# All gated output rows of the mixers as seven block products, in another order of the seven

## The chip, the cores and the metric

The kernel runs on one core of a Trainium2 chip. The metric is the device time of one execution in microseconds (us). Engines are named as in the profile: PE (matrix multiplies; PEld is its weight load), DVE (vector), ACT (scalar: copies, casts and activations), POOL (here mostly DMA issue) and SP (DMA issue). Each engine works through its own instructions in order and waits at semaphores for the others.

## The reference, cut to what matters

The program is one step of a two-layer encoder on 640 rows (512 prompt frames and 8 x 16 sample frames), in fp32. A layer is a feed-forward half step, a mixer, and a second feed-forward half step. The change lies in the mixer:

```python
z = h @ w_in                      # h: 640 x 1024; columns: conv B, C, V | q, k, v | gates
g = sigmoid(z[gates] + b_gate)    # 2048 gate columns
g_conv, g_attn = split(g, 2)
m = g_conv * (y_conv @ w_conv_out) + g_attn * (y_attn @ w_attn_out)   # y: 640 x 512, w: 512 x 1024
x = x + m @ w_o
```

## The kernel before, in words

Everything is kept transposed: 128 features on the partitions, the 640 rows along the free dimension, in two halves `t1` and `t2` of 320. A fp32 product is made of three fp32r matmuls: weights and operands are each split into `hi` (an ACT cast to fp32r) and `lo` (a DVE subtraction), and `hi*hi`, `hi*lo`, `lo*hi` are summed in PSUM.

**Products by seven.** For the gates, the kernel takes the weights of a pair of output blocks and a pair of input blocks as a 2 x 2 matrix, the activations (two input blocks by two halves) as another, and forms the 2 x 2 product with seven block products instead of eight. The seven are named by their operand: `11`, `21`, `22` are quarters of the activations as they are; `N6`, `T5`, `T7`, `T4` are differences of quarters. A unit of this kind ("mix") reads two weight tiles of 128 x 1024 and turns them into four slabs: slab 0 holds the weights of products 11 and 21, slab 1 those of N6 (first half, from sums `s`) and T5 (second half, from `raw`), slab 2 those of T7 (`one`, which POOL adds up by DMA) and 22, slab 3 those of T4. Per unit PE issues 7 x 12 matmuls of 320 columns, 84 in all.

**Stage.** The function `outputs` is the last part of each mixer, after attention, and is run once for each of the two layers. Its instructions on PE, DVE and ACT stand in the order in which the code is written (`tc.manual_schedule` with all three engines), so that order is what each engine follows. It consists of gate pairs `gate_pair(2)` to `gate_pair(14)` (seven units by seven), and of the gated output rows between them: 8 rows of `co` (conv) and 8 of `ao` (attention). Rows 4 to 7 of each are made by `rows`, one unit by seven for four output rows. Rows 0 to 3 are made singly by `out`: four plain products on the operands `yc` or `ya`, 24 matmuls, into one PSUM tile `py`. After the stage, the `w_o` products `po` read its result `mo`.

**Weights run ahead.** `prep(i)` has ACT cast slab `i` into `whi`; `flush()` has DVE form `wlo`. `slab()` hands out the next slab and prepares the one two further on; `quiet()` hands one out and prepares nothing. `source()` has DVE add up raw tiles (`raw`, `s`) where a slab is a sum. There are three buffers each of `whi` and `wlo`.

**Names in the trace.** `qa`, `qb`, `qc` are the three PSUM banks of a gate pair: bank a takes 11, then N6, T7 and T4; b takes 21; c takes T5, then 22. ACT copies bank a out after 11 (`capsm`, below "copy c1") and after N6 (`capsm` again, "copy u2"), and bank c after T5 (`c`). Only then may N6, T7 and 22 add to those banks. `ra..`, `rb..`, `rc..` are the same for `rows`, with copies into `capsm` or `rs`; the copy of bank a after N6 is `rs<-raco`. `rrm` is the norm's factor, `g` the gates, `mm` the output rows, `sm` the gate bias of the sigmoids (`ACTIVATE g<-g,sm`). Sigmoids are held back in `lates` and issued by `due()` after copy c1 of the next unit.

The two functions that the diff touches, `mixer_order` (the order of the weights in memory) and `outputs`:

Of the kernel before, what the change touches and what calls it, by code (L numbers as in the profile page):

```python
# [16 lines left out]
P = 128  # L17
# [170 lines left out]
def two(ps):  # L188
    return ps[:, :, :HT]
# [7 lines left out]
def trunk(ctx: ExitStack, tc: tile.TileContext, xin, wst, small, pbias, samplebias, kcache, vcache, gfin,  # L197
# [1299 lines left out]
    def outputs(l, gp, X, st, cs, ycp, yas, sigmoid, gates):  # L1497
# [4 lines left out]
        ycs = [z[:, i] for z in ycp for i in range(2)]  # L1502
        mm = [spare[i // 2][:, i % 2] for i in range(CT)] + ycs
# [14 lines left out]
        def gate_pair(m, at):  # L1518
# [6 lines left out]
            u, g = gates[m], gates[m + 1] = tmp(f"g{n}"), tmp(f"g{n}_1")  # L1525
            prep(used[0] + 1)
            flush()
            at[0]()
# [8 lines left out]
            at[1]()  # L1537
# [6 lines left out]
            at[2]()  # L1544
# [8 lines left out]
            block(pa, s3, 0, XT4, every, False, True)  # L1553
            DVE.tensor_tensor(out=g[:, t1], in0=pa, in1=rr[:, t1], op=ALU.mult)
            lates.append(lambda: sigmoid(g, m + 1, -1.0))
            flush()

        def parts(pool, tag, name, src):
            hi, lo = (pool.tile([P, T], F32R, tag=f"{tag}{i}", name=f"{name}{i}") for i in ("hi", "lo"))
            split(hi, lo, src)  # L1560
            return hi, lo

        def out(m, y, then=None, post=None):

            due()
            py = acc(f"py{l}_{m}")
            product(py, y)
            if then:
                then()
            g = gates[m]  # L1570
            if m < KT:
                DVE.tensor_tensor(out=halves(mm[m]), in0=two(py), in1=halves(g), op=ALU.mult)
            else:
                DVE.tensor_tensor(out=halves(g), in0=two(py), in1=halves(g), op=ALU.mult)
                add(mm[m - KT], mm[m - KT], g)
            flush()
            if post:
                post()

        yc, ya = [], []  # L1580
        mo = [None] * KT
        srcs = [yas[:, c, :] for c in range(CT)]
        x, moves = {}, []

        def take(y, name, cs, srcs):
            for c in cs:
                y.append(parts(gp, f"y{c}", f"{name}{l}_{c}", srcs[c]))

        def take_even(c):
            y = tuple(gp.tile([P, T], F32R, tag=f"y{c}{i}", name=f"ya{l}_{c}{i}") for i in ("hi", "lo"))  # L1590
            split(*(z[:, t1] for z in y), srcs[c][:, t1])
            ya.append(y)

        def low(lo, z, hi):
            DVE.tensor_tensor(out=lo, in0=z, in1=hi.bitcast(F32), op=ALU.subtract)

        def room(name):
            for k in EXTRA:
                x[name, k] = tuple(gp.tile([P, 2, HT], F32R, tag=f"x{EXTRA.index(k)}{i}",
                                           name=f"x{i}{name}{l}_{EXTRA.index(k)}") for i in ("hi", "lo"))  # L1600

        def minus(out, a):
            DVE.scalar_tensor_tensor(out=out, in0=a, scalar=-1.0, in1=out, op0=ALU.mult, op1=ALU.subtract)

        def mixed(i):

            z = ycp[i].rearrange("p c (a b) -> p (c a) b", a=2)
            e1, e2, o1, o2 = (z[:, k] for k in range(4))
            add(e1, e1, e2, ALU.subtract)
            add(e2, o2, e2, ALU.subtract)  # L1610
            minus(o2, e1)
            minus(o1, o2)
            yield
            for k in EXTRA:
                ACT.copy(x["co", k][0][:, i], z[:, 1 + EXTRA.index(k)])
            yield
            for k in EXTRA:
                hi, lo = (u[:, i] for u in x["co", k])
                low(lo, z[:, 1 + EXTRA.index(k)], hi)
            yield  # L1620
            hi, lo = (u[:, t2] for u in yc[2 * i])
            ACT.copy(hi, e1)
            yield
            low(lo, e1, hi)
            yield

        za = yas.rearrange("p (i c) (a b) -> p i (c a) b", i=2, a=2)

        def mix(n):

            e1, e2, o1, o2 = (za[:, :, k] for k in range(4))
            if n == 0:
                add(e1, e1, e2, ALU.subtract)
            elif n == 1:
                add(e2, o2, e2, ALU.subtract)
            else:
                minus(*((o2, e1) if n == 2 else (o1, o2)))

        def place(k):
            if k == XT5:  # L1640
                return [(*(u[:, t2] for u in ya[2 * i]), za[:, i, 0]) for i in range(2)]
            return [(*x["ao", k], za[:, :, 1 + EXTRA.index(k)])]

        def high(*ks):
            for k in ks:
                for hi, _, z in place(k):
                    ACT.copy(hi, z)

        def rest(*ks):
            for k in ks:  # L1650
                for hi, lo, z in place(k):
                    low(lo, z, hi)

        EXTRA = XT7, XT4, XN6

        def kind(name, i, k):
            if k in EXTRA:
                return tuple(z[:, i] for z in x[name, k])
            hi, lo = (yc if name == "co" else ya)[2 * i + (k in (X21, X22))]
            return tuple(z[:, t2 if k in (X22, XT5) else t1] for z in (hi, lo))  # L1660

        def rows(name, ms, first, mid=None, late=None, end=False, defer=False):

            n = f"{name}{l}_{ms[0]}"
            gs = [gates[m + (KT if name == "ao" else 0)] for m in ms]
# [3 lines left out]
            s1, s2, s5 = stage  # L1669

            def mul(ps, s, half, k, start):
                for u in range(2):
                    for i in range(2):
                        kp = half * NP + 2 * u + i
                        wh, wl = (z[:, kp * P : (kp + 1) * P] for z in s)
                        xh, xl = kind(name, i, k)
# [13 lines left out]
            def moved(r):  # L1690
                for u in range(2):
                    ACT.copy(mm[ms[2 * r + u]], gs[2 * r + u])

            w = quiet()
            mul(a, w, 0, X11, True)
            ACT.copy(s1, two(A))
# [8 lines left out]
            flush()  # L1705
            mul(a, w, 0, XN6, False)
            ACT.copy(s2, two(A))
            gated(0, [s1[:, u] for u in range(2)], t1)
            if mid:
                mid()  # L1710
            mul(c, w, 1, XT5, True)
            for u in range(2):
                ACT.copy(s5[:, u], c[u])
            w = slab(True)[0]
            mul(a, w, 0, XT7, False)
# [3 lines left out]
            if defer:  # L1719
                moves.append(lambda: gated(1, [s5[:, u] for u in range(2)], t2, -1.0))  # L1720
            else:
                gated(1, [s5[:, u] for u in range(2)], t2, -1.0)
            if late:
                late()
            mul(c, w, 1, X22, False)
# [4 lines left out]
            mul(a, w, 0, XT4, False)  # L1730
# [3 lines left out]
            if name == "co":  # L1734
                lates.append(lambda: moved(0))
                moves.append(lambda: moved(1))
            if end:
                flush()

# [12 lines left out]
        none = lambda: None  # L1752

        def going(*zs):
            return lambda: [next(z) for z in zs]

        gate_pair(2, [none, none, lambda: take(yc, "yc", range(CT), ycs)])
        z = [mixed(i) for i in range(2)]
        room("co")
        out(0, yc, None, going(z[0]))  # L1760
        out(1, yc, None, going(*z))
        out(2, yc, None, going(*z))
        out(3, yc, None, going(z[1]))
        gate_pair(4, [going(*z), going(*z), none])
        gate_pair(6, [none] * 3)
        rows("co", (4, 5, 6, 7), None)
        gate_pair(8, [none, moves[0], lambda: take(ya, "ya", range(CT), srcs)])
        room("ao")
        out(8, ya, None, lambda: mix(0))
        out(9, ya)  # L1770
        gate_pair(10, [lambda: mix(1), lambda: (mix(2), high(XT7)), lambda: (mix(3), rest(XT7))])
        out(10, ya)
        out(11, ya)
        gate_pair(12, [none, lambda: high(XN6, XT4), lambda: (rest(XN6, XT4), high(XT5))])
# [664 lines left out]
```

## Time and profile before

| what | value |
|---|---|
| median of 3 runs (lowest, highest) | 2481.88 us (2481.07 to 2482.76) |
| span of the profiled execution | 2479.9 us |
| busy: PE, DVE, ACT, POOL | 99%, 88%, 56%, 13% of the span |
| HBM read | 239.48 MB |

The profiled execution's own time is its span, from the first instruction to the last; the timed runs lie 2.0 us above it at the median. "Busy" counts a time in which at least one instruction of the engine was under way. Matmuls overlap, so that PE at 99% says that PE hardly ever stood still, and nothing of how full it was.

### The profile page before, as it was taken

The numbers are of one execution on the slowest core, as the hardware profiler recorded it, in microseconds if no ns is written. First come the engines' busy times: TensorE is split into PE (matmuls) and PEld (weight loads), VectorE is DVE, ScalarE is ACT, GpSimd is POOL, SyncE is SP. The second block draws the span as 40 slices with busy tenths as digits, with TensorE's granted clock in tenths as the row PEclk, the third lists the DMA queues.
The fourth block names the chain that finished last, engine by engine and source line by source line (L and its number), as shares of the span: only waits on it lengthen the run. The fifth ranks groups of instructions, "written<-read, shape, count | busy, mean of one in ns | idle before, by whom it ended". The sixth has DMA issues, their size and how long they took to land.

```text
span 2479.9 us, 44056 instructions
## 1 busy us (share of the span) xinstructions
PE 2466.4 (99%) x17264; PEld 2414.6 (97%) x17264; DVE 2182.6 (88%) x3644; ACT 1386.7 (56%) x2231; POOL 320.8 (13%) x483
## 2 busy tenths in 40 slices
PE   9999999999999999999999999999999999999999
PEld 8999999889999999999999999998899999999998
DVE  7999998888888899998799999988888889999997
ACT  6555555665555555555665555566655556555555
POOL 0211112211000001111001010121110000111111
PEclk9999999999999999999999999999999999999999
DMA  4443444335344234444334343452453432444444
GB/s 155 128 120 101 124 117 120 114 110 175 102 118 123 93 102 107 112 118 119 109 94 109 110 117 102 117 128 102 138 167 94 119 119 92 108 113 107 112 117 117
DMA packets 113520, 288.16 MB, mean 116 GB/s; under 512 B 12992, under 2 KB 52544, under 8 KB 113312
## 3 DMA queue, kind: packets, MB, share of 16 engines
q1 hardware_dynamic: 69552, 220.10, 27.0%
q0 software_dynamic: 43328, 64.99, 13.8%
q8 instruction: 135, 2.21, 0.4%
q14 instruction: 73, 0.60, 0.1%
q10 hardware_dynamic: 432, 0.25, 0.0%
HBM read 239.48 MB, written 7.94 MB: 100 GB/s over the span
## 4 chain that ended last, share of the span: by engine, by line
PE 91%; DVE 4%; issue 3%; ACT 1%; DMA 1%; DVEq 0%; SPq 0%; ACTq 0%; POOLq 0%
PE pab L459 12%; PE paa L459 10%; PE pcb L459 6%; PE daa L1147 5%; PE dab L1147 5%; PE pca L459 5%; PE po L435 5%; PE qa L459 4%; PE pbb L459 3%; PE dca L1147 3%; PE dcb L1147 2%; PE pba L459 2%; PE ma_cv L459 2%; PE ma_qk L459 2%; PE py L435 2%
## 5 line engine op out<-in xcount | busy, mean ns | idle before, releaser
L364 ACT CAST whi<-raw 128x1024 fp32r<-128x1024 f32 (+1 forms) x578 | 502.3, 874 | 373.4 <-PE pbb L459 46.3
L369 DVE TENSOR_TENSOR wlo<-raw,whi 128x1024 fp32r<-128x1024 f32 (+1 forms) x578 | 577.0, 1001 | 135.4 <-ACT whi L364 131.2
L364 ACT CAST whi<-s 128x1024 fp32r<-128x1024 f32 (+1 forms) x162 | 152.9, 944 | 319.4 <-DVE s L296 113.5
L459 PE MATMUL pab<-xhib,whi 128*128 128x320 f32 x704 | 217.7, 309 | 0.0
L459 PE MATMUL pab<-xhib,wlo 128*128 128x320 f32 x704 | 217.2, 309 | 0.0
L459 PE MATMUL pab<-xlob,whi 128*128 128x320 f32 x704 | 217.2, 309 | 0.0
L459 PE MATMUL paa<-xhia,whi 128*128 128x320 f32 x640 | 197.8, 309 | 0.2 <-DVE ga L296 0.2
L459 PE MATMUL paa<-xhia,wlo 128*128 128x320 f32 x640 | 197.5, 309 | 0.0
L459 PE MATMUL paa<-xloa,whi 128*128 128x320 f32 x640 | 197.5, 309 | 0.0
L369 DVE TENSOR_TENSOR wlo<-s,whi 128x1024 fp32r<-128x1024 f32 (+1 forms) x162 | 176.3, 1088 | 4.0 <-ACT whi L364 4.0
L1169 POOL DMA_DIRECT2D x<-c_a x80 | 69.9, 1021 | 575.9 <-ACT ahia L1051 205.5
L1169 POOL DMA_DIRECT2D x<-c_b x72 | 63.2, 1014 | 583.1 <-ACT ahib L1051 205.4
L459 PEld LDWEIGHTS pab<-xhib,whi 128*128 128x128 f32 x704 | 132.1, 188 | 0.9 <-issue 0.9
L459 PEld LDWEIGHTS pab<-xhib,wlo 128*128 128x128 f32 x704 | 132.1, 188 | 0.0
L459 PEld LDWEIGHTS pab<-xlob,whi 128*128 128x128 f32 x704 | 132.1, 188 | 0.0
L459 PEld LDWEIGHTS paa<-xhia,whi 128*128 128x128 f32 x640 | 120.1, 188 | 1.1 <-DVE ga L296 0.4
L459 PEld LDWEIGHTS paa<-xloa,whi 128*128 128x128 f32 x640 | 120.1, 188 | 0.3 <-DVE xloa L703 0.3
L459 PEld LDWEIGHTS paa<-xhia,wlo 128*128 128x128 f32 x640 | 120.1, 188 | 0.1
L296 DVE TENSOR_TENSOR raw<-s,raw 128x512 f32<-128x512 f32 x162 | 110.7, 683 | 0.0
L459 PE MATMUL pcb<-xhib,wlo 128*128 128x320 f32 x352 | 108.8, 309 | 0.0
L459 PE MATMUL pcb<-xlob,whi 128*128 128x320 f32 x352 | 108.6, 309 | 0.0
L459 PE MATMUL pcb<-xhib,whi 128*128 128x320 f32 x352 | 108.6, 309 | 0.0
(909 smaller groups left out, 8201.3 us busy)
## 6 DMA issues: line engine op xcount, KB each, us to landing
raw<-in_wst SPq DMA_DIRECT2D x375, 512.0 KB, 3.5
x<-c_a POOLq DMA_DIRECT2D x80, 160.0 KB, 4.8
x<-c_b POOLq DMA_DIRECT2D x72, 160.0 KB, 4.2
lent<-in_wst POOLq DMA_DIRECT2D x36, 256.0 KB, 3.7
kc<-in_kcache SPq DMA_DIRECT2D x32, 256.0 KB, 4.8
vc<-in_vcache SPq DMA_DIRECT2D x16, 512.0 KB, 4.3
one<-in_wst POOLq DMA_DIRECT2D x32, 256.0 KB, 4.0
x<-u_a POOLq DMA_DIRECT2D x40, 160.0 KB, 4.1
```

The source lines that it names most:

```text
L296: DVE.tensor_tensor(out=out, in0=a, in1=b, op=op)
L364: ACT.copy(hi[:, d], src[:, c])
L369: DVE.tensor_tensor(out=lo, in0=src, in1=hi.bitcast(F32), op=ALU.subtract)
L435: PE.matmul(ps[:, a, :HT], w, x[a] if isinstance(x, tuple) else x[:, a * HT : (a + 1) * HT], start=first and j == 0 and not seeded, stop=l ...
L459: PE.matmul(ps, a, b, start=start and kp == 0 and j == 0, stop=stop and kp == NP - 1 and j == 2, skip_group_check=True)
L1147: PE.matmul(ps[u], w, y, start=start and i == 0 and j == 0, stop=i == 1 and j == 2, skip_group_check=True)
L1169: POOL.dma_start(x[ms[2 * u + r]][:, cols], z[:, u], accum_op=ALU.add)
```

## The change

Rows 0 to 3 of `co` and `ao` are made by `rows` too, so that `out`, its plain products and its operands are gone. `rows` takes the seven in the order 11, T5, N6, 21, T7, 22, T4 (before: 11, 21, N6, T5, T7, 22, T4). It takes slab 1 with `quiet()`, and its weights of slab 3 are cast after product 21. In every `rows` but a layer's first, ACT writes product 11 into bank b, and 21 is added to it there ("seeds a bank"), in place of an addition by DVE. The operands of both groups are made by a class `Mixed`, in eight steps, handed to the gate pairs and the first `rows` of the group as hooks `at[0..3]`: after the cast of slab 2, after the copies u2 and c, before product 22, and at the end. In `gate_pair`, `flush()` now stands ahead of the last product with `rrm`. The sums `total(0..3)` of conv and attention rows move into gate pairs 12 and 14. Gates 2, 3, 6 and 7 are written into the tiles of the output rows, so that two of the four rows' copies `moved` fall away.

```diff
@@ mixer_order
-    out += gates[:2] + [("co", m) for m in range(4)] + gates[2:4] + [("rows", ("co", (4, 5, 6, 7)))]
-    for i in range(2):
-        out += [gates[4 + i], ("ao", 2 * i), ("ao", 2 * i + 1)]
-    out += gates[6:] + [("rows", ("ao", (4, 5, 6, 7)))]
+    rows = [("rows", (name, ms)) for name in ("co", "ao") for ms in ((0, 1, 2, 3), (4, 5, 6, 7))]
+    out += gates[:3] + rows[:1] + gates[3:4] + rows[1:2] + gates[4:6] + rows[2:3] + gates[6:] + rows[3:]
@@ outputs, gate_pair
             prep(used[0] + 1)
             flush()
-            at[0]()
+            call(at, 0)
             block(pb, s0, 1, X21, every, True, True)
...
             block(pa, s3, 0, XT4, every, False, True)
+            flush()
             DVE.tensor_tensor(out=g[:, t1], in0=pa, in1=rr[:, t1], op=ALU.mult)
             lates.append(lambda: sigmoid(g, m + 1, -1.0))
-            flush()
+            call(at, 3)
@@ outputs, class Mixed (new)
+            def high(self, i, *whats):
+                for what in whats:
+                    hi, _, z = self.part(i, what)
+                    ACT.copy(hi, z)
+            def low(self, i, *whats):
+                for what in whats:
+                    hi, lo, z = self.part(i, what)
+                    DVE.tensor_tensor(out=lo, in0=z, in1=hi.bitcast(F32), op=ALU.subtract)
+            def mix(self, i, *ks):
...
+            def steps(self):
+                hi, lo, mix = self.high, self.low, self.mix
+                return [[f] for f in (
+                    lambda: (mix(0, "T5"), hi(0, "11", "T5"), lo(0, "11")),
+                    lambda: (mix(1, "T5"), hi(1, "11", "T5"), lo(0, "T5")),
+                    lambda: (lo(1, "11", "T5"), hi(0, "2")),
+                    lambda: (lo(0, "2"), hi(1, "2")),
+                    lambda: (mix(0, "N6"), hi(0, "N6"), lo(1, "2")),
+                    lambda: (mix(1, "N6"), hi(1, "N6"), lo(0, "N6"), mix(0, "T7", "T4")),
+                    lambda: (lo(1, "N6"), hi(0, "T")),
+                    lambda: (mix(1, "T7", "T4"), hi(1, "T"), lo(0, "T"), lo(1, "T")))]
@@ outputs, rows
             w = quiet()
-            mul(a, w, 0, X11, True)
-            ACT.copy(s1, two(A))
+            mul(a, w, 0, "11", True)
+            ACT.copy(two(B) if seed else s1, two(A))
             due()
             prep(used[0] + 1)
             flush()
-            if first:
-                first()
-            mul(b, w, 1, X21, True)
-            add(s1, two(B), s1)
-            w = slab(True)[0]
-            flush()
-            mul(a, w, 0, XN6, False)
-            ACT.copy(s2, two(A))
-            gated(0, [s1[:, u] for u in range(2)], t1)
-            if mid:
-                mid()
-            mul(c, w, 1, XT5, True)
+            call(at, 0)
+            w1 = quiet()
+            mul(c, w1, 1, "T5", True)
             for u in range(2):
                 ACT.copy(s5[:, u], c[u])
+            mul(a, w1, 0, "N6", False)
+            ACT.copy(s2, two(A))
+            mul(b, w, 1, "21", not seed)
+            prep(used[0] + 1)
+            if not seed:
+                add(s1, two(B), s1)
+            gated(0, b if seed else [s1[:, u] for u in range(2)], t1)
+            flush()
+            call(at, 1)
             w = slab(True)[0]
-            mul(a, w, 0, XT7, False)
+            mul(a, w, 0, "T7", False)
...
@@ outputs, the stage's order
+        yc = Mixed("co", [quarters(z) for z in ycp])
+        at = yc.steps()
+        gate_pair(2, at[:4])
+        gate_pair(4, at[4:7])
+        rows(yc, (0, 1, 2, 3), at[7:])
+        gate_pair(6)
+        rows(yc, (4, 5, 6, 7))
+        ya = Mixed("ao", [quarters(yas[:, 2 * i : 2 * i + 2]) for i in range(2)])
+        at = ya.steps()
+        gate_pair(8, at[:4])
+        gate_pair(10, at[4:7])
+        rows(ya, (0, 1, 2, 3), at[7:])
+        gate_pair(12, [[lambda: total(0)], [lambda: total(1)], [lambda: total(2)]])
+        gate_pair(14, [[lambda: total(3)], [lambda: (begun(*range(4)), given(0, 2))]])
+        rows(ya, (4, 5, 6, 7), [[], [lambda: given(1, 3)]], True)
```

How the instructions stand, at three places of the first layer.

PE, where product 11 of `rows` for co rows 4 to 7 ends (weights `whi_7802` and `wlo_7803` are slab 0), before:

```order
L1678 MATMUL raco_4_7862<-yc_2lo,whi_7802 128x320
L1678 MATMUL raco_4_7862<-yc_2hi,wlo_7803 128x320
L1678 MATMUL rbco_4_7861<-yc_1hi,whi_7802 128x320
L1678 MATMUL rbco_4_7861<-yc_1lo,whi_7802 128x320
L1678 MATMUL rbco_4_7861<-yc_1hi,wlo_7803 128x320
```

The same place after (`whi_7813`, `wlo_7814` are slab 0, `whi_7852` and `wlo_7853` slab 1):

```order
L1643 MATMUL raco_4_7873<-y1co_1lo,whi_7813 128x320
L1643 MATMUL raco_4_7873<-y1co_1hi,wlo_7814 128x320
L1643 MATMUL rcco_4_0_7874<-y4co_0hi,whi_7852 128x320
L1643 MATMUL rcco_4_0_7874<-y4co_0lo,whi_7852 128x320
L1643 MATMUL rcco_4_0_7874<-y4co_0hi,wlo_7853 128x320
```

The second of the seven now reads slab 1, 12 matmuls after the unit's start, where before it read slab 0 again.

ACT, in gate pair 8, from copy c1 to the copy of bank c, before (`whi_8019` is slab 2, `whi_8038` slab 3):

```order
L1523 COPY capsm_4819<-qa_8_7998 128x320
L1692 COPY yc_0_4821<-g_4_7613 128x640
L1692 COPY yc_0_4821<-g_4_1_7614 128x640
L364 CAST whi_8019<-one_7822 128x512
L364 CAST whi_8019<-raw_7933 128x512
L364 CAST whi_8038<-raw_7952 128x512
L1534 COPY capsm_4819<-qa_8_7998 128x320
L1536 COPY c_4831<-qc_8_8000 128x320
```

After (`y1ao_0hi`, `y4ao_0hi` are operands of products 11 and T5):

```order
L1525 COPY capsm_4819<-qa_8_8020 128x320
L1657 COPY yc_0_4821<-g_4_0_7478 128x640
L1657 COPY yc_0_4821<-g_4_1_7479 128x640
L362 CAST whi_8041<-one_7833 128x512
L362 CAST whi_8041<-raw_7943 128x512
L1592 CAST y1ao_0hi<-ya_4762 128x320
L1592 CAST y4ao_0hi<-ya_4762 128x320
L362 CAST whi_8064<-raw_7962 128x512
L1536 COPY capsm_4819<-qa_8_8020 128x320
L1538 COPY c_4831<-qc_8_8022 128x320
```

Two operand casts stand between the casts of slabs 2 and 3 and so ahead of copy u2; the second of them reads what DVE mixes in the same step.

ACT, from the end of gate pair 2 into the next unit, before (the next unit is the plain products `out`):

```order
L364 CAST whi_7425<-raw_7394 128x1024
L1354 ACT_TABLE_LOAD
L1354 ACTIVATE g_0_7126<-g_0_7126,sm 128x640
L1354 ACTIVATE g_1_7127<-g_1_7127,sm 128x640
L1354 ACTIVATE g_2_7324<-g_2_7324,sm 128x640
```

After (the next unit is gate pair 4, and `capsm<-qa_4` its copy c1):

```order
L362 CAST whi_7436<-s_94_7417 128x512
L362 CAST whi_7436<-raw_7412 128x512
L1352 ACT_TABLE_LOAD
L1352 ACTIVATE g_0_7126<-g_0_7126,sm 128x640
L1352 ACTIVATE g_1_7127<-g_1_7127,sm 128x640
L1592 CAST y2co_1hi<-yc_1_4822 128x640
L1525 COPY capsm_4819<-qa_4_7460 128x320
```

The load of the sigmoids' table, two sigmoids and an operand cast now stand right ahead of a copy that product N6 waits for.

More of the change, by code (lines that the diff above doesn't have):

```diff
@@ L1580, in outputs @@
[L1580 to L1642, printed above, removed]
@@ L1666, in rows @@
+        seeded = [False]
+        def rows(y, ms, at=(), end=False):
+            n = f"{y.name}{l}_{ms[0]}"
+            co = y.name == "co"
+            gs = [gates[m + (0 if co else KT)] for m in ms]
             B, A = (acc(f"r{i}{n}") for i in "ba")
@@ L1718, in rows @@
             ahead()
[L1719 to L1725, printed above, removed]
+            gated(1, [s5[:, u] for u in range(2)], t2, -1.0)
+            call(at, 2)
+            mul(c, w, 1, "22", False)
             for u in range(2):
@@ L1750, in given, with quarters @@
                 split(*mo[m], mm[m])
[L1752 to L1774, printed above, removed]
-        pre = lambda: rest(XT5)
-        gate_pair(14, [pre, lambda: (begun(*range(4)), given(0, 2)), none])
-        rows("ao", (4, 5, 6, 7), None, lambda: given(1, 3), None, True)
+        def quarters(z):
+            return z.rearrange("p c (a b) -> p (c a) b", a=2)
+        yc = Mixed("co", [quarters(z) for z in ycp])
[13 more added lines that the diff above has]
+        rows(ya, (4, 5, 6, 7), [[], [lambda: given(1, 3)]], True)
         begun(*range(4, KT))
```

97 lines of the change are left out of this document (49 added, 48 removed).

## The prediction

> **What bounds the kernel now.** I read the page first, then the stage `outputs` of each layer (product 11 of gate pair 2 to the first `po`), then groups, then single transitions.
>
> ```profile
> span 2479.9 us, 44056 instructions
> PE 2466.4 (99%) x17264; PEld 2414.6 (97%) x17264; DVE 2182.6 (88%) x3644; ACT 1386.7 (56%) x2231; POOL 320.8 (13%) x483
> PE 91%; DVE 4%; issue 3%; ACT 1%; DMA 1%; DVEq 0%; SPq 0%; ACTq 0%; POOLq 0%
> one<-in_wst POOLq DMA_DIRECT2D x32, 256.0 KB, 4.0
> ```
>
> PE is busy for 99% of the span and is 91% of the chain that ended last. So a matmul less counts in full, and so does any wait of PE that is new. The windows show the stage in both layers:
>
> ```profile
> core 0: us, PE busy (x) PEld busy (x) DVE busy (x) ACT busy (x) POOL busy (x), PEclk, DMA share, GB/s
> 635.00:774.30 139.30, 139.25 (x950) 138.95 (x949) 120.73 (x195) 79.91 (x133) 8.60 (x12) 1.00 0.36 106
> 1863.56:2002.82 139.26, 139.21 (x950) 138.91 (x950) 120.59 (x195) 79.76 (x133) 8.64 (x12) 1.00 0.35 107
> ```
>
> PE never rests, at clock 1.00. The code has 9 units of 84 matmuls and 8 `out` of 24, 948 in all (the windows touch two more): 139.30 / 948 = 0.147 us each, 1.76 for a block of 12, 12.34 for a unit. DVE rests for 18.6 us of the stage, ACT for 59.4. The layers agree within 0.04 us, so I work out the first and double it.
>
> **What falls away.** Per layer 8 x 24 matmuls go and 2 x 84 come: 24 fewer, 24 x 0.147 = 3.53 us. One wait that PE has now goes with the old order; it also shows what a late `wlo` costs (gate pair 14, product N6):
>
> ```profile
> 752.60 0.68 DVE L369 TENSOR_TENSOR wlo<-s,whi 128x512 fp32r<-128x512 f32 x1
> 752.97 0.31 PE L459 MATMUL qa<-tlo,whi 128*128 128x320 f32 x1
> 753.33 0.41 PE L459 MATMUL qa<-thi,wlo 128*128 128x320 f32 x1
> ```
>
> `wlo` ends at 753.28, the matmul that reads it starts 0.05 later and takes 0.41 instead of 0.31: a wait costs its length, 0.05, and 0.10 to start again. Due at 753.12, it lost 0.21 + 0.10 = 0.31. Credit per layer: 3.53 + 0.31 = 3.84.
>
> **What DVE, ACT and the queues get.**
>
> ```profile
> L369 DVE TENSOR_TENSOR wlo<-raw,whi 128x512 fp32r<-128x512 f32 x26 | 17.8, 685 | 0.5
> L369 DVE TENSOR_TENSOR wlo<-raw,whi 128x1024 fp32r<-128x1024 f32 x14 | 17.1, 1219 | 0.9 <-ACT whi L364 0.9
> L296 DVE TENSOR_TENSOR g<-qa,c 128x320 f32<-128x320 f32 x7 | 3.4, 491 | 12.4 <-PE qa L459 12.4
> L1685 DVE TENSOR_TENSOR g<-capsm,g 128x320 f32<-128x320 f32 x4 | 1.8, 484 | 0.0
> L236 DVE TENSOR_TENSOR yc_0lo<-yc,yc_0hi 128x640 fp32r<-128x640 f32 x1 | 0.8, 819 | 0.0
> L1615 ACT CAST xhico<-yc 128x320 fp32r<-128x320 f32 x6 | 2.5, 458 | 2.8 <-DVE yc L296 2.2 <-DVE yc L1603 0.6
> ```
>
> Counted over the listings, DVE gets for both layers 60 more instructions of 320 columns, 32 more of 512, 4 fewer of 1024 and 28 fewer of 640 (sums and splits of weights against evacuations of `py`; the seeded bank saves 640-column additions in this count and is never waited for). By the rows that is 29.0 + 21.9 - 4.9 - 22.9 = 23.1 us; neighbours overlap by 0.08 (a 512 of 0.68 follows the next after 0.60), so 60 x 0.08 less, 18.3, or 9.1 per layer. It fits in the 18.6 that DVE rests, and ACT's 30 more (7 us per layer) in 59.4. POOL gets 4 DMAs more per layer, a unit ahead of use, 4.0 us to landing: hidden by 12.34 of PE. SP's list keeps its 469 instructions: 0. The moved sums `total(0..3)` stand where DVE rests before T7 (12.4 us over 7 gate pairs): 0, or if a chain is hit 0.74 once. So no engine is full; the question is what stands in a queue ahead of what PE needs. I found four such places.
>
> **1. T5 second, in all four `rows`.** Gate pair 6 and the `rows` behind it, before:
>
> ```profile
> 686.01 0.31 PE L1678 MATMUL raco<-yc_0hi,whi 128*128 128x320 f32 x1
> 687.43 0.48 DVE L1554 TENSOR_TENSOR g<-qa,rrm 128x320 f32<-128x320 f32 x1
> 688.43 0.68 DVE L369 TENSOR_TENSOR wlo<-raw,whi 128x512 fp32r<-128x512 f32 x1
> ```
>
> The second half of slab 1's `wlo`, which T5 needs, ends at 689.11. It hangs on T7 of the gate pair (DVE waits there, 12.4 us in the group above), so an idle DVE does not bring it forward. `flush()` put ahead of the `rrm` product takes 0.40 off: 688.71. T5's third matmul, the first with `wlo`, is due 14 matmuls after 686.01, at 688.07: PE loses 0.64 + 0.15 = 0.8. Behind gate pairs 4 and 10 a 320 split (0.40) stands in between: 1.2. Behind 14 two 640 splits come ahead of the chain: between 0.8 and 1.5, I take 1.2. Sum 4.4 per layer; bounds 2.6 (0.64 each) and 6.0.
>
> **2. Copy u2 behind operand casts, gate pairs 8, 10, 4.** Gate pair 8, before:
>
> ```profile
> 701.86 0.62 ACT L364 CAST whi<-one 128x512 fp32r<-128x512 f32 x1
> 703.40 1.15 ACT L364 CAST whi<-raw 128x512 fp32r<-128x512 f32 x2 [0.92 <-DVE raw L296]
> 704.45 0.42 ACT L1534 COPY capsm<-qa 128x320 f32<-128x320 f32 x1
> 704.06 0.69 DVE L369 TENSOR_TENSOR wlo<-raw,whi 128x512 fp32r<-128x512 f32 x1
> 704.67 0.48 DVE L296 TENSOR_TENSOR g<-qb,capsm 128x320 f32<-128x320 f32 x1
> 705.36 0.31 PE L459 MATMUL qa<-thi,whi 128*128 128x320 f32 x1
> 640.48 0.43 ACT L1534 COPY capsm<-qa 128x320 f32<-128x320 f32 x1 [1.15 <-PE qa L459]
> 642.04 0.31 PE L459 MATMUL qa<-thi,whi 128*128 128x320 f32 x1
> ```
>
> Copy u2 ends at 704.87, T7 starts at 705.36: 0.49 to spare. After, the mix for T5 stands on DVE behind that `wlo<-raw` (704.67 to 705.15), ACT's cast of it ends at 705.64 at the earliest (0.46), the cast of slab 3 at 706.17, u2 at 706.50 (each starts 0.09 before the last one's end): 1.14 + 0.15 = 1.3. In gate pair 10 the same, with a 640 split more ahead on DVE and sigmoids for copies: 1.5. In gate pair 4, behind place 3, c1, two sigmoids, two casts, two `wlo`, mix, cast, cast and u2 follow each other, 5.1 us where 3.53 are there: 1.7. Gate pair 2 (last two rows) has 1.13 to spare, one mix and two casts less a rest of 1.15 on ACT: 0. Sum 4.5; bounds 2.7 and 5.8 (a 640 split more in 4 and 10).
>
> **3. Table load ahead of c1, gate pair 4.** A gate pair behind a gate pair before (4 to 6), and ACT at the end of pair 2:
>
> ```profile
> 673.71 0.31 PE L459 MATMUL qa<-hhim,whi 128*128 128x320 f32 x1
> 674.59 0.62 ACT L364 CAST whi<-raw 128x512 fp32r<-128x512 f32 x1
> 645.45 0.72 ACT L235 CAST yc_3hi<-yc 128x640 fp32r<-128x640 f32 x1
> 647.15 1.28 ACT L1354 ACT_TABLE_LOAD   x1
> 648.44 1.55 ACT L1354 ACTIVATE g<-g,sm 128x640 f32<-128x640 f32 x2
> 700.28 0.43 ACT L1523 COPY capsm<-qa 128x320 f32<-128x320 f32 x1 [0.67 <-PE qa L459]
> ```
>
> Before, all this ran beside `out`, which waits for none of it. Now ACT is through with slab 1's casts 1.50 after the unit's start (675.21 - 673.71), then table 1.28, two sigmoids 1.55, cast 0.72, c1 0.43, less overlaps of 0.09: 5.30. N6 is due after 24 matmuls, 3.53: 1.77 + 0.15 = 1.9; bounds 1.2 (the cast earlier) and 1.9. [...]
>
> **4. Copy of bank a behind operand casts, first `rows` of co and ao.** `rows` before:
>
> ```profile
> 690.56 1.15 ACT L364 CAST whi<-raw 128x512 fp32r<-128x512 f32 x2
> 691.31 0.69 DVE L369 TENSOR_TENSOR wlo<-raw,whi 128x512 fp32r<-128x512 f32 x1
> 691.61 0.69 ACT L1707 COPY rs<-raco 128x640 f32<-128x640 f32 x1
> 693.05 0.31 PE L1678 MATMUL raco<-xhico,whi 128*128 128x320 f32 x1
> ```
>
> The last step puts two mixes behind that `wlo` (to 692.8), a 640 cast (to 693.6), then the two copies of bank c (0.34 each) and the copy of bank a (0.69): 694.9. T7, due at 693.05, is put off to 694.25 by place 1: 0.65 + 0.15 = 0.8. A sigmoid that place 1 delays adds up to 0.3; I take 1.0 each. Sum 2.0; bounds 0.6 and 2.2.
>
> **Sum.** 4.4 + 4.5 + 1.9 + 2.0 = 12.8 lost, 3.84 won: 9.0 per layer, 18 for two. The profiled span would go from 2479.9 to 2497.9; the runs' median lies 2.0 above the span, so 2481.9 + 18 = 2500. With all lower bounds 7.1 - 3.84 = 3.3 per layer: 2488. With all upper ones, 15.9, and 1 us where waits push each other: 13 per layer, 2508.
>
> **Rivals.**
> - *Faster: lead.* ACT rests 59.4 us per stage; were its operand casts and copies through before PE asks, none of the four would remain: -7.7, 2474. It wins if the waits of a layer stay under 3.84. [...] Against: u2's 0.49 to spare is less than one mix and two casts in a row, and place 1 hangs on T7. Chance 0.08.
> - *Even: only T5's order counts.* Place 1 stays, 4.4 - 3.84 = 0.6 per layer: 2483. Speaks for it that DVE's row is shown, while ACT's positions are counted on; against, that ACT's rows are as plain. Chance 0.09.
> - *DVE full.* If DVE keeps its 18.6 of rest and gets 9.1 more, the stage takes 148.4 instead of 139.3: again 18 in all, by another road; above that, with waits chaining into the `w_o` products, 2510 and more. Chance 0.08.
>
> **Chances and range.** My case, 2488 to 2508: 0.75. What a measurement of this kernel can just tell from no change is about 0.2%, 5 us: faster 0.08, same 0.09, slower 0.83 (mine and the third). 2487 to 2511 leaves out less than 0.2.
>
> **What the changed profile would show.** Stages of about 148 us instead of 139.3, with 924 matmuls; PE waits in `rc..` (T5) for DVE `wlo`, in `qa` (N6 of pair 4, T7 of 4, 8, 10) for ACT `capsm`, in `ra..` (T7) for ACT `rs`; DVE near 130 busy per stage. I am wrong if ACT's casts of `y4..` don't wait for DVE, if T5 starts on time, or if PE waits elsewhere, as for an operand's `lo` in T7 or for `mo` in the `po` products.

## The result and the profile after

The changed kernel takes 2501.64 us (median, 2500.65 to 2502.69) against 2481.6 for the kernel before in runs on the same chip: a ratio of 1.0081, interval 1.0066 to 1.0096. It is slower by 20 us. Of the page, after, the span, the engines and the chain that ended last; then the windows of the two stages, with the columns shown before:

```profile
span 2499.7 us, 44058 instructions
PE 2465.2 (99%) x17216; PEld 2407.4 (96%) x17216; DVE 2201.1 (88%) x3704; ACT 1398.5 (56%) x2261; POOL 326.6 (13%) x491
PE 85%; DVE 8%; ACT 3%; issue 2%; DMA 1%; SPq 0%; DVEq 0%; ACTq 0%; POOLq 0%
```

```profile
634.31:784.93 150.62, 139.61 (x926) 135.65 (x925) 131.00 (x227) 86.04 (x148) 11.46 (x16) 1.00 0.37 105
1873.90:2022.70 148.80, 138.65 (x926) 135.52 (x925) 129.79 (x225) 85.84 (x148) 11.50 (x16) 1.00 0.39 107
```

PE runs 48 matmuls fewer in all and still reads 99% busy: a matmul is shown 0.31 us long where the next one starts 0.147 after it, so the profile covers 0.16 us of each wait. What tells is the chain, where PE fell from 91% to 85% and DVE and ACT rose from 5% to 11%. The stages grew from 139.30 and 139.26 us to 150.62 and 148.80, 20.9 together. The rest of the span is 0.96 shorter (its start by 0.69, the stretch between the stages by 0.27, the tail not at all): 19.9, and the spans differ by 19.8.

What PE waited for in the first stage, in microseconds, times and longest (the same view of the kernel before has no row there at all):

```profile
PE qa L457 <- ACT capsm L1536: 4.1, 5, 1.2
PE qa L457 <- ACT capsm L1525: 1.7, 1, 1.7
PE rcao L1643 <- DVE wlo L367: 1.6, 2, 0.9
PE rcco L1643 <- DVE wlo L367: 1.5, 2, 1.0
PE raao L1643 <- ACT rs L1671: 0.7, 1, 0.7
PE raco L1643 <- ACT rs L1671: 0.7, 1, 0.7
PE rcao L1643 <- ACT whi L362: 0.4, 1, 0.4
PE raao L1643 <- DVE rs L294: 0.4, 1, 0.4
```

L1525 is copy c1 and L1536 copy u2 of a gate pair, L1671 the copy of bank a in `rows`, L367 and L362 the low and the high part of a slab. The pitch is the time from the start of one matmul to the start of the next, 0.147 us where nothing waits. Measured from start to start, less the pitch, a wait costs about 0.16 more than this view gives (the view counts from the end of the matmul before, and matmuls overlap), and the first matmul behind it loses another 0.10. Two of these waits in the timeline (start, length, engine, line, and in brackets the idle time before):

```profile
652.81 0.41 PE L457 MATMUL qa<-thi,whi 128*128 128x320 f32 x1 [1.66 <-ACT capsm L1525]
666.39 0.42 PE L1643 MATMUL rcco<-y4co_0hi,wlo 128*128 128x320 f32 x1 [0.95 <-DVE wlo L367]
```

The first cost 1.82 + 0.10, the second 1.11 + 0.11. Summed so, the first stage has 15.2 us of waits, the second 13.4. With 924 products of 0.1466 (12.32 us for a unit of 84 without a wait) that is 150.7 and 148.9, against 150.62 and 148.80 in the windows: the waits are the whole difference.

### The profile page after: what moved, and what is told of

Same layout as the page of the kernel before. It is cut to its first block, busy times and chain, and to the rows that moved or that the text cites. A ratio compares the mean times of both kernels' runs of the same rounds, so it can differ in the third digit from the quotient of the medians.

```text
span 2499.7 us, 44058 instructions
## 1 busy us (share of the span) xinstructions
PE 2465.2 (99%) x17216; PEld 2407.4 (96%) x17216; DVE 2201.1 (88%) x3704; ACT 1398.5 (56%) x2261; POOL 326.6 (13%) x491
## 4 chain that ended last, share of the span: by engine, by line
PE 85%; DVE 8%; ACT 3%; issue 2%; DMA 1%; SPq 0%; DVEq 0%; ACTq 0%; POOLq 0%
PE pab L457 12%; PE paa L457 11%; PE pcb L457 6%; PE daa L1145 6%; PE pca L457 5%; PE dab L1145 5%; PE po L433 5%; PE pbb L457 3%; DVE wlo L367 3%; PE dca L1145 3%; PE pba L457 3%; PE dcb L1145 2%; PE ma_cv L457 2%; PE ma_qk L457 2%; PE pv L1792 2%
## 5 line engine op out<-in xcount | busy, mean ns | idle before, releaser
L362 ACT CAST whi<-raw 128x1024 fp32r<-128x1024 f32 (+1 forms) x586 | 505.4, 867 | 368.4 <-PE pbb L457 47.2
L367 DVE TENSOR_TENSOR wlo<-raw,whi 128x1024 fp32r<-128x1024 f32 (+1 forms) x586 | 580.2, 992 | 137.1 <-ACT whi L362 133.0
L362 ACT CAST whi<-s 128x1024 fp32r<-128x1024 f32 (+1 forms) x166 | 155.3, 936 | 344.9 <-DVE s L294 138.5
L367 DVE TENSOR_TENSOR wlo<-s,whi 128x1024 fp32r<-128x1024 f32 (+1 forms) x166 | 179.0, 1078 | 4.0 <-ACT whi L362 4.0
```

What stands on the lines that cost most here:

```text
L362: ACT.copy(hi[:, d], src[:, c])
L367: DVE.tensor_tensor(out=lo, in0=src, in1=hi.bitcast(F32), op=ALU.subtract)
```

## The experiments

Places 1 to 4 are those of the prediction. The first four runs undo one place each; what each saved is against 2501.64. The runs below were on other chips, where the kernel before took 2480.97 to 2481.70 us, so half a microsecond between two of them says nothing.

### Place 3: the table load earlier

```
+            if m == 2:
+                for i in range(2):
+                    sigmoid(gates[i], i)
             block(pc, s2, 1, X22, every, False, True)
...
-            if m == 2:
-                for i in range(2):
-                    sigmoid(gates[i], i)
```

> The sigmoids of gates 0 and 1, and with them the load of their table, are issued before product 22 of gate pair 2 instead of at its end, so that they no longer stand ahead of copy c1 of gate pair 4. Theory (four places in the queues): the wait before N6 of gate pair 4 goes, 1.82 + 0.10 us in each layer, nothing else changes: span 2499.7 - 3.8 = 2496. Rival (DVE is full, the waits are only where its lateness shows): the instructions are the same, so the span stays at 2499 to 2500. Rival (waits pass on): T7 of the same pair waits 1.9 longer, span 2499.5.

2496.48 us (ratio to before 1.0062, 1.0047 to 1.0077): 5.2 us saved. N6 of gate pair 4 waits no more. ACT ahead of it, in this run:

```profile
644.93 1.28 ACT L1352 ACT_TABLE_LOAD   x1
646.23 1.55 ACT L1352 ACTIVATE g<-g,sm 128x640 f32<-128x640 f32 x2
...
649.35 0.41 ACT L1525 COPY capsm<-qa 128x320 f32<-128x320 f32 x1
```

In the changed kernel the load began at 648.98 and c1 at 652.35. The other rows of the wait view stayed as they were, but for one wait less of copy u2 (gate pair 2): this place stood by itself. The spans of the two profiled executions differ by 4.6.

### Place 2: the casts behind copy u2

`mix` forms an operand's difference on DVE, `hi` casts an operand on ACT, `lo` makes its low part on DVE. A slot is one of the hooks `at[0..3]`.

```
-                    lambda: (mix(0, "T5"), hi(0, "11", "T5"), lo(0, "11")),
-                    lambda: (mix(1, "T5"), hi(1, "11", "T5"), lo(0, "T5")),
+                    lambda: mix(0, "T5"),
+                    lambda: (hi(0, "11", "T5"), mix(1, "T5"), hi(1, "11", "T5"), lo(0, "11", "T5")),
...
-                    lambda: (mix(0, "N6"), hi(0, "N6"), lo(1, "2")),
-                    lambda: (mix(1, "N6"), hi(1, "N6"), lo(0, "N6"), mix(0, "T7", "T4")),
+                    lambda: (mix(0, "N6"), lo(1, "2")),
+                    lambda: (hi(0, "N6"), mix(1, "N6"), hi(1, "N6"), lo(0, "N6"), mix(0, "T7", "T4")),
```

> The casts that a mix in slot 0 feeds (T5 and 11, N6) are issued in slot 1, behind copies u2 and c, with the same number of instructions on every engine. Theory: the waits before T7 of gate pairs 4, 8 and 10 go, 1.51 + 1.22 + 1.52 in each layer, and 0.73 in pair 2 of the first: span 2499.7 - 9.2 = 2490.5. Rival (DVE full): no change, 2499 to 2500. Rival (waits pass on): place 1 and place 4 take it, 2497 or more.

2498.84 us (1.0071, 1.0056 to 1.0086): 2.8 saved of the 9.2 expected, so the rival "waits pass on" (2497 or more) held. What PE waited for in its first stage, the rows that changed most:

```profile
PE qa L457 <- ACT capsm L1536: 0.3, 1, 0.3
PE qa L457 <- DVE g L294: 0.3, 1, 0.3
PE rcao L1643 <- ACT whi L362: 0.8, 2, 0.4
```

The row of copy u2 fell from 4.1 to 0.3, as expected. But T4 of gate pair 10 now waits for DVE, and T5 of ao's first rows (in the second stage of co's too) waits for a slab's high part (0.4) before it waits for `wlo`. Part of what was taken away came back one place on. A stretch at half pitch, told of at the end, took 1.6 us more.

### Place 1: the rows in the order before

The seeded bank goes too, so DVE adds product 11 again; of the edit, the order:

```
-            mul(c, w1, 1, "T5", True)
...
-            mul(a, w1, 0, "N6", False)
-            ACT.copy(s2, two(A))
-            mul(b, w, 1, "21", not seed)
+            mul(b, w, 1, "21", True)
+            add(s1, two(B), s1)
+            w = slab(True)[0]
+            flush()
+            mul(a, w, 0, "N6", False)
+            ACT.copy(s2, two(A))
...
+            mul(c, w, 1, "T5", True)
```

> The seven of every rows unit in the order 11, 21, N6, T5, T7, 22, T4 again, without the seeded bank (DVE adds product 11 in three more units per layer, 0.74 us each). Theory: T5 no longer waits, 4.9 us per layer less, but T7 of the first rows units is due about 1.1 earlier while its copy comes 0.7 earlier, 0.4 us more in each: 2 x (4.9 - 0.8) = 8.2 less, span 2491.5. Rival (DVE full): 4.4 us more DVE work in all, span 2504.

2495.6 us (1.0058, 1.0041 to 1.0075): 6.0 saved of the 8.2 expected. In the first stage:

```profile
PE raco L1639 <- ACT rs L1667: 1.7, 1, 1.7
PE raao L1639 <- ACT rs L1667: 1.7, 1, 1.7
```

No product waits for `wlo` any more. T7 of the first rows, put off before by T5's wait, now waits 1.7 for the copy of bank a where it waited 0.7. Behind one of these waits, 13 matmuls at half pitch took 1.6 us more.

### Place 4: a cast behind the copy of bank a

```
-                    lambda: (mix(1, "T7", "T4"), hi(1, "T"), lo(0, "T"), lo(1, "T")))]
+                    lambda: (mix(1, "T7", "T4"), lo(0, "T")), lambda: None, lambda: None,
+                    lambda: (hi(1, "T"), lo(1, "T")))]
...
             ACT.copy(s2, two(A))
+            call(at, 3)
```

> In the first rows unit of co and ao the cast of T7 and T4 for the second pair is issued behind the copy of bank a, and its split with it. Theory: the wait before T7 goes, 0.92 + 0.93 in each layer, unless the split now comes late for T7's fifth matmul (up to 0.3 each): span 2499.7 - 3.7 = 2496, at most 2497.2. Rival (DVE full): 2499 to 2500.

2499.29 us (1.0073, 1.0058 to 1.0088): 2.4 saved of 3.7. The two rows of L1671 are gone. In the second layer 1.35 us of it was lost again where the stage begins, in a wait for ACT's part of the attention before it; I did not follow that up.

### Place 1 again, by DVE's queue alone

`u` is the first of a gate pair's two gates; DVE scales it by `rr` ahead of the low part that T5 needs.

```
             s3 = slab(True)[0]
-            DVE.tensor_tensor(out=u, in0=u, in1=rr, op=ALU.mult)
...
             block(pa, s3, 0, XT4, every, False, True)
             flush()
+            DVE.tensor_tensor(out=u, in0=u, in1=rr, op=ALU.mult)
```

> The changed kernel with one line moved in all seven gate pairs: gate u's scaling by rr (0.83 us of DVE) is issued behind the low part of the next slab, no longer ahead of it. Order of products, seed and all DVE work stay. Theory (place 1 is a place in DVE's queue): T5 of the four row groups waits 0.3 to 0.5 us where it waited 1.22, 0.82, 1.21 and 1.63 us (with restarts), about 2.8 us less a layer: 2496 us. Rival 'DVE full' (the loss is the sum of DVE's work, which is the same here): the waits show up elsewhere, 2501.6 us, give or take 2.

2500.24 us (1.0075, 1.0058 to 1.0092): 1.4 saved, not 5.6, as the rival "DVE full" had it (2501.6, give or take 2). The first stage:

```profile
PE raao L1643 <- ACT rs L1671: 1.7, 1, 1.7
PE raco L1643 <- ACT rs L1671: 1.7, 1, 1.7
...
PE rcao L1643 <- DVE wlo L367: 0.3, 1, 0.3
```

T5 waits 0.29 + 0.11 at the first rows, where it waited 1.11 + 0.11, so the position in DVE's queue was its cause. But T7, three blocks of 12 on, waits 1.0 us longer. The wait had moved, not gone.

### All four places, and two more versions

The next kernel joins the first four edits. The one after it adds: casts of N6 a slot later, T7's and T4's mixes at the end of the gate pair, `total(3)` and two of the last splits earlier. The third is that one with the changed kernel's order and seed, and u's scaling behind the low part.

> All four places at once: sigmoids of gates 0 and 1 early, operand casts behind copy u2, rows in the order before (11, 21, N6, T5, no seeded bank), the second pair's last cast behind the copy of bank a. DVE's work is that of the changed kernel but for four adds. Single gains seen were 5.2, 2.8, 6.0 and 2.4 us, 16.4 together, by which 2485 us. Theory (waits of places that pass on to each other go when both go): T5 of the first rows no longer waits 1.8 us, T7 no longer 2.0; a stage is 924 products of 0.147, 135.8 us, and some 2 us of waits that are left (T4 of gate pairs 4 and 10, T4 of the last rows): 138 us, span 2477, 2479 us. Rival 'DVE full': DVE keeps its rest, a stage stays at 147 us or above, 2497 us.

> As the one before, and besides: pair 1's casts of N6 one slot later, the mixes of T7 and T4 at the end of the gate pair, total(3) at the end of gate pair 12 and the splits of m1 and m3 earlier (gate pair 14 and the start of the last rows). Theory: the waits of T4 of gate pairs 4 and 10 (0.3 to 0.4 us) and of the last rows (0.4 to 0.6) go too: a stage of 136.5 to 137, 2476.5 us, 5 us less than the kernel before. Rival 'DVE full': 2497 us.

> As the one before, but with the changed kernel's own order of products in the rows (11, T5, N6, 21, T7, 22, T4) and its seeded bank; instead gate u's scaling is issued behind the low part of the next slab. Theory: the order of the products costs only what T5 still waits, 0.3 to 0.5 us in each of four row groups, 1.2 to 2 us a layer: 2479 to 2481 us. Rival 'the order itself costs' (T5 second cannot be fed in time in any issue order): 1.2 us a row group as in the changed kernel, 2486 us or more. Rival 'DVE full': 2497 us.

2493.03 us (1.0046, 1.0031 to 1.0060), 2499.12 (1.0070, 1.0055 to 1.0085) and 2496.73 (1.0062, 1.0047 to 1.0077). All three expectations failed, by 14, 23 and 16 us; the rival's 2497 lay nearer each time. The rows of the first of them:

```profile
PE raco L1640 <- DVE y4co_1lo L1597: 1.4, 1, 1.4
PE raao L1640 <- DVE y4ao_1lo L1597: 1.4, 1, 1.4
PE raao L1640 <- DVE y4ao_0lo L1597: 0.8, 1, 0.8
PE raco L1640 <- DVE y4co_0lo L1597: 0.8, 1, 0.8
```

Of the old waits, 0.2 to 0.3 us is left in a few spots. T7 of the first rows now waits for the operand's own low parts, a wait that the prediction had named as a sign against it; in the changed kernel it is not there, it came with these edits. On DVE ahead of the first of them:

```profile
665.06 0.69 DVE L367 TENSOR_TENSOR wlo<-one,whi 128x512 fp32r<-128x512 f32 x1 [0.81 <-ACT whi L362]
667.08 0.82 DVE L1597 TENSOR_TENSOR y4co_0lo<-yc,y4co_0hi 128x640 fp32r<-128x640 f32 x1
```

From 642.29 to 664.25 DVE had rested no longer than 0.12 us at a time; then it stood still for 0.81, because ACT's cast came late. So both a backlog on DVE and the order of the queues are in this wait. The other two kernels lose most at a new spot, N6 of the first rows, for ACT's copy after product 11 (2.6 us each in the first of the two, 1.6 in the second). In the first, that copy (at 664.95) stands behind an operand cast that the edit had put there, and the cast waits for a mix that comes late on DVE (the wait view, then ACT's timeline):

```profile
PE raco L1640 <- ACT capsm L1658: 2.6, 1, 2.6
...
664.32 0.72 ACT L1592 CAST y4co_0hi<-yc 128x640 fp32r<-128x640 f32 x1 [2.85 <-DVE yc L1606]
```

So I divided the stage by what it works on: the two gate pairs with an operand's steps and the first rows behind them, for co and for ao, against what follows. Before, the windows of the two operand stretches (264 products each):

```profile
635.00:673.75 38.75, 38.75 (x267) 38.75 (x266) 33.25 (x55) 21.70 (x36) 1.43 (x2) 1.00 0.30 93
698.33:737.10 38.77, 38.77 (x267) 38.77 (x266) 36.11 (x58) 21.78 (x35) 2.87 (x4) 1.00 0.41 115
```

After, the same stretches and the two that follow them (252, 168, 252 and 252 products):

```profile
634.31:677.68 43.37, 38.40 (x253) 37.07 (x253) 37.97 (x66) 26.04 (x44) 2.86 (x4) 1.00 0.32 93
677.68:703.14 25.46, 24.92 (x170) 24.65 (x169) 20.18 (x36) 13.41 (x23) 2.87 (x4) 1.00 0.45 126
703.14:744.96 41.82, 38.02 (x255) 36.97 (x253) 38.12 (x69) 24.67 (x44) 4.29 (x6) 1.00 0.42 118
744.96:784.93 39.97, 38.27 (x255) 36.96 (x253) 34.73 (x59) 21.92 (x37) 1.43 (x2) 1.00 0.31 94
```

The fourth number is DVE's busy time. The change took 12 products from each operand stretch, which leaves PE 252 x 0.147 = 37.05 us, and put work on DVE, which now has 38 us there, 1 more than PE. Over a whole stage DVE rests for 19 to 20 us; here it would have nothing to spare if PE did not wait. With all four edits the ao stretch was 41.59 us, 0.2 shorter than after the change, though hardly any of the old waits is in it. (The co stretch was 43.36 us, but 21 of its matmuls ran at half pitch, some 2.5 us.)

### Less work for DVE, and its work elsewhere

Two kernels test that. One is the kernel with all four places mended, without gate u's scaling in the four gate pairs of the operand stretches. The other is complete: places 1 and 3 undone, the second pair's mixes and the first pair's low part moved up in `rows`, and ao's T5 mixes made in the second rows of co.

```
-            DVE.tensor_tensor(out=u, in0=u, in1=rr, op=ALU.mult)
+            if m not in (2, 4, 8, 10):
+                DVE.tensor_tensor(out=u, in0=u, in1=rr, op=ALU.mult)
```

> The kernel with all four places mended, but gate u of gate pairs 2, 4, 8 and 10 is left unscaled (its product with rr, 0.83 us of DVE, is left out in each), which alters the output and nothing of the order. New theory: from gate pair 2 to the end of the first rows (and from pair 8) PE has 252 products of 0.147 = 37.05 us and DVE 38 to 39 us of work, so DVE runs behind there and every wait that is taken away comes back further on; that stretch took 43.4 and 41.6 us. With 1.66 us less of DVE's work it is 1.7 us shorter where DVE alone decides and up to 4.5 where the stretch at half pitch goes too: four such stretches, 7 to 15 us in all, 2478 to 2486 us, 2483 taken. Rival (the order of ACT's queue, copies behind casts, holds PE there): the stretch keeps its length, 2490 us or more.

2488.3 us (1.0028, 1.0018 to 1.0038), 4.7 below the kernel with all four places, and 2 above the range that I gave. Part of the 4.7 is that it ran less at half pitch (told of at the end). In the first stage's ao stretch neither has any; its windows are, first with all four mended, then with less work:

```profile
702.18:743.77 41.59, 38.64 (x254) 36.99 (x253) 38.56 (x71) 24.44 (x44) 4.28 (x6) 1.00 0.44 120
```

```profile
699.39:738.45 39.06, 37.48 (x255) 36.95 (x254) 36.90 (x69) 24.35 (x44) 4.29 (x6) 1.00 0.48 127
```

1.66 us of DVE's work less made the stretch 2.53 shorter. The 0.87 between the two numbers is about as long as a wait of DVE for a weight tile that the run with less work does not have there:

```profile
714.42 0.69 DVE L294 TENSOR_TENSOR raw<-raw 128x512 f32<-128x512 f32 x1 [0.94 <-DMA raw<-in_wst]
```

So DVE's work seems to count in full in this stretch. It is not all that counts: one wait did not move, T7's fifth matmul for `y4ao_1lo`, 1.52 us in both. That is the cast which place 4's edit had put behind the copy: in the old order of products it comes too late, a place that I had made myself.

The edit of the other, beside those of places 1 and 3:

```
-                    lambda: (mix(1, "T7", "T4"), hi(1, "T"), lo(0, "T"), lo(1, "T")))]
+                    lambda: (mix(1, "T7", "T4"), lo(0, "T")), lambda: hi(1, "T"), lambda: lo(1, "T"))]
...
+            call(at, 0)
             due()
+            call(at, 1)
             prep(used[0] + 1)
             flush()
-            call(at, 0)
+            call(at, 2)
...
-        rows(yc, (4, 5, 6, 7))
+        rows(yc, (4, 5, 6, 7), [[], [], [], [lambda: ya.mix(0, "T5")], [lambda: ya.mix(1, "T5")]])
```

> Complete again: sigmoids of gates 0 and 1 early and the rows in the order before, as in the runs that did the one and the other alone; besides, in the rows the second pair's mixes and the first pair's low part ahead of the sigmoids and the next slab, its cast behind the sigmoids, and ao's two T5 mixes (0.48 us each) moved ahead into the rows of co, where DVE has 2 us to spare. Single gains 5.2 and 6.0 us would give 2490.4. Theory of DVE's backlog: T7 of the first rows waits less than 1.9 us, the stretch of co stays at 40 to 41 us (DVE's work, 38 us, and its start), that of ao falls from 41.8 to about 40.5, the last rows lose 1.7 us of waits: 2485 to 2489 us, 2487 taken. Theory of the four places alone: a stage of 137 us and what copy u2 costs (4.3): 2484 us or less, T7 of the first rows without a wait.

2485.17 us (1.0016, 1.0007 to 1.0025): 16.5 saved. That is the lower edge of what the backlog gave (2485 to 2489), and 1 above what the four places alone gave (2484 or less), so the time does not decide between the two. The co stretch, the part of it from T7 of gate pair 2 on, and the waits of the first stage:

```profile
633.96:673.37 39.41, 37.74 (x255) 36.95 (x253) 37.10 (x64) 26.39 (x44) 2.86 (x4) 1.00 0.33 100
643.49:673.37 29.88, 28.41 (x193) 27.89 (x191) 29.36 (x50) 19.98 (x33) 2.86 (x4) 1.00 0.36 110
```

```profile
PE qa L457 <- ACT capsm L1536: 3.4, 5, 1.2
PE raao L1639 <- ACT rs L1669: 0.3, 1, 0.3
PE raao L1639 <- DVE rs L294: 0.2, 1, 0.2
PE raco L1639 <- ACT rs L1669: 0.2, 1, 0.2
```

The trace tells more than the time. From T7 of gate pair 2 to the end of co's first rows DVE is busy for 29.36 of 29.88 us, where PE's 193 matmuls at 0.147 would take 28.4. So in this version DVE's work does set the length of that part. Place 2 is the largest of the waits left: T7 of gate pairs 4, 8 and 10 behind copy u2, at 1.38, 0.68 and 1.38, with restarts 3.8 of the 6.7 us in the first stage and of the 5.6 in the second.

### Trying for the rest

Both kernels build on the last one. The first makes gate pair 4's scaled u only at the end of co's first rows, and ao's `11` parts in co's second rows. The second also gives `gate_pair(4, ...)` and `gate_pair(10, ...)` an empty first slot, so that no cast stands ahead of u2.

> The kernel of early mixes, and more of DVE's work moved out of the two full stretches: gate pair 4's scaling of u (0.83 us, and its sigmoid on ACT) waits until the end of the first rows of co, and ao's casts and low parts of '11' (0.96 us of DVE) are made in the second rows of co. T7 of gate pairs 4 and 10 still waits 1.4 to 1.5 us for the copy u2 behind a cast on ACT. Theory of both causes: those two waits stay, T7 of the first rows (0.52 us in each) waits no more, gate pair 8 loses its 0.8: stages of 140 to 141 us, 2482 us. If DVE's backlog were not what holds the first rows: 2485 us as before this step.

> As the one before, and in gate pairs 4 and 10 the mixes, casts and low parts of the operand one slot later, so that the copy u2 has no cast ahead of it. Theory of both causes: with the backlog smaller, the 1.5 us of T7 in each of the two pairs go and at most half of them come back in the first rows: stages of 138 to 139.5 us, 2477 to 2480 us, less than the kernel before (2481.0). Rival (DVE's backlog is still as long, so the waits only move into the first rows, as with the casts moved alone): 2482 us or more.

2484.66 us (1.0015, 1.0006 to 1.0023) and 2485.93 (1.0021, 1.0012 to 1.0030): no gain, and both expectations missed (for the second, the rival's 2482 or more held). The first came out at the 2485 that was named for the case that the backlog does not hold the first rows. Its trace says otherwise for co: T7 of co's first rows waits no more, and the co stretch is 38.41 and 38.89 us in the two stages (39.41 and 39.05 before this step). But where the work went it cost time: a late `wlo` in gate pair 8 (0.49), and 0.4 more between the two stretches in each stage. In the second, PE waits in the first stage for:

```profile
PE raao L1647 <- DVE y4ao_1lo L1605: 0.8, 1, 0.8
PE raco L1647 <- ACT rs L1677: 0.7, 1, 0.7
PE raao L1647 <- ACT rs L1677: 0.7, 1, 0.7
PE qa L457 <- DVE wlo L367: 0.5, 2, 0.3
```

Of copy u2's 3.0 us 2.6 went and these came, for nearly the same sum (5.95 us of waits in the first stage, 6.17 in the run before). No version of the twelve is faster than the kernel before.

## Why the prediction was right, and where its reasons fell short

- **Credit.** 924 products in the stage at an unchanged pitch, as forecast. The old 0.31 us wait did not stay away altogether: gate pair 14 waits 0.12 at N6 and 0.41 at T7 in the first stage, and not in the second.
- **Place 1** (4.4 forecast): T5 lost 1.22, 0.82, 1.21 and 1.63, in sum 4.88, restarts counted. The last was larger than forecast (1.2) for a reason not seen: T5's first matmul there waits for a high part (0.60) ahead of `wlo`. That `wlo`'s position in DVE's queue was the cause is shown by the run that moved u's scaling; that undoing it would give the time back is not so, since T7 took it.
- **Place 2** (4.5): 1.51, 1.22 and 1.52 in gate pairs 4, 8 and 10, 4.25. Gate pair 2 was put at 0 and lost 0.84 in the first stage, nothing in the second.
- **Place 3** (1.9): 1.92. Undone, it gave 5.2 us over both stages (4.6 by the spans), more than 2 x 1.92: the wait in gate pair 2 was absent in that run too. The measured wait agrees with the 1.28 us that the load's row gives before and after; in the changed kernel the first sigmoid starts 0.02 behind its end.
- **Place 4** (2.0): 0.92 and 0.93, 1.85.
- **The sum.** The four places cost 12.9 a layer against 12.8 forecast. Missed were the T4 of the last rows behind the sum into `rs` (0.60), and in the first stage alone gate pairs 2 and 14 (1.6). A forecast of 18 became 19.8.
- **The step that fell short** is "It fits in the 18.6 that DVE rests". The total was right: 131.0 and 129.8 busy against about 130. But much of the added work lies in two stretches of 37 us, where DVE had 5.5 and 2.7 us of rest before. There it is a second limit, just behind the four places. The rival "DVE full" asked whether DVE is full over the stage; it is full over long parts of about half of it. By that much the rival held: with all four places mended its 2497 was nearer to the 2493 measured than my 2479. That run is no clean test, though: in its profiled execution some 6 us are half pitch and 6.1 (4 x 1.52) the cast that I had misplaced. As it was put, with DVE keeping its 18.6 of rest, the rival is out. The stages after the change do agree with it (19.6 and 19.0 of rest), but with DVE's work nearly unchanged (132.03 us in the first stage) the best version rests 10.1 us there, and gave back 16.5 of 20 us.
- **Lead and T5's order alone**, the two rivals with lower times, are out: a stage has 15.2 and 13.4 us of waits, not under 3.84, and undoing place 1's order gave 6.0 us of the 20.

What stays open: whether the last 3 to 4 us over the kernel before can be won by an order at all, or only by less work on DVE in the two stretches. Why some waits appear in one layer's stage and not in the other's was not tried either.

## What to carry to other kernels

Price a change by its places in the queues: here each of the four places, read from a spare time and a row of durations, came out within 0.5 us, and the waits that no place had named were 2.8 us in all. But when you mend such a place, ask first what the engine behind it has left *in that stretch*, not in the stage; a wait that hides a backlog comes back further on (with u's scaling moved, T5 of the first rows waited 0.8 us less and T7 1.0 more), and a stretch's length tells this sooner than its list of waits. Saved matmuls (7 us here) are worth only what the engines that feed them can keep up with.

## What the hardware showed that I had not expected

After some waits PE ran at half pitch (0.267 us from start to start instead of 0.147) for 2.4 to 5.6 us. In the kernel with all four places, behind three waits close together (0.36, 1.09 and 1.52 us, all within 3.8), in the timeline and in the windows:

```profile
670.01 0.64 PE L1640 MATMUL raco<-y4co_1lo,whi 128*128 128x320 f32 x1 [1.36 <-DVE y4co_1lo L1597]
...
671.24 0.47 PE L1640 MATMUL raco<-y4co_0hi,wlo 128*128 128x320 f32 x1
671.51 0.47 PE L1640 MATMUL raco<-y4co_1hi,whi 128*128 128x320 f32 x1
```

```profile
671.00:676.00 5.00, 5.00 (x20) 5.00 (x20) 3.34 (x5) 0.00 (x0) 0.86 (x1) 0.50 0.52 126
```

The granted clock is 0.50 there, instead of 1.00. In that kernel half pitch struck three of four first rows, 50 matmuls at 0.12 more each, 6 us of its span; its runs spread from 2489 to 2496. In the run with the casts behind u2 it followed a single wait of 1.96 us (granted clock 0.54 from 653 to 656), and not the one of 1.97 in the second stage. In the run with the old order it followed one of four waits of 1.89 or 1.90, in the second of the three versions three of four waits of 2.7, and in the run with u's scaling moved none of four waits of 1.87 or 1.88. Why the same wait is followed by half pitch in one place and not in another, no run here shows. So a wait near 2 us cost nearly twice its length in one stage (1.96, and 13 matmuls at 0.12 more), and in the other stage of that run no half pitch followed.
